# Prompt attention scores from rounded parts: queries and keys divided in two, three products for one

## The chip, the cores and the metric

The kernel runs on one core of a Trainium2 chip. The metric is the device time of one execution in microseconds; the kernel before takes 1125.41 us, the median of three runs (1124.91 to 1126.1). "Faster" and "slower" in this document mean a difference that such a measurement can tell from none.

The engines are named as in the profile: PE is TensorE (PEld its weight loads), DVE is VectorE, ACT is ScalarE, POOL is GpSimd, SP is SyncE, which here only issues transfers.

## The reference, cut to what matters

One layer of a hybrid decoder runs for a prompt of 512 tokens (with 16 learned meta tokens ahead of it) and for eight samples of 8 new tokens. Everything is float32. The change touches only the scores of the prompt's differential attention: four heads, two maps of 64 dimensions each.

```python
DA_HEADS = 4; DA_HEAD_DIM = 64; Q_BLOCK = 128; N_META = 16; SEQ = 512

def diff_attn_prompt(q, k, v, lam):            # q, k: (1, 528, 4, 2, 64)
    ...
    def one_block(args):                       # one block of 128 queries
        q_blk, start = args                    # q_blk is q * 64 ** -0.5
        q_pos = start + jnp.arange(Q_BLOCK)
        s = jnp.einsum('bqhmd,bkhmd->bhmqk', q_blk, k, preferred_element_type=jnp.float32)
        s = jnp.where(k_pos[None, :] <= q_pos[:, None], s, -jnp.inf)
        pr = jax.nn.softmax(s, axis=-1)
        a = pr[:, :, 0] - lam * pr[:, :, 1]    # the difference of the two maps
        return jnp.einsum('bhqk,bkhe->bqhe', a, vf)
```

The queries and keys come out of one input projection, h = rmsnorm(x) @ w_in, whose next columns give the values, the gated DeltaNet's inputs and the gates. After the attention follow the DeltaNet's chain, the merge of the branches, an output projection and a ConvFFN. The new keys and values are outputs too.

## The kernel before

**Rounded parts.** Nearly all large products of this kernel are made from a format that TensorE takes in one instruction, fp32r (F32R in the code). A float32 array is divided into a rounded part and the rest: `split` (L330) casts on ScalarE (L331) and subtracts on VectorE or GpSimd (L332). `project` (L366) and its like then add three products in PSUM: rounded x rounded, rounded x rest, rest x rounded. Products of plain float32 operands are taken as two instructions each. In the profile both formats show as f32 in a matmul's form; the tile names tell them apart: xhi, xlo, whi, wlo are parts, qT and kT are plain float32.

**Queries (`da_queries`, L1243).** The embedded input lies in SBUF as parts, transposed, in two stretches of columns: 256 columns and the rest. For each of four heads a projection of 128 columns of w_in fills two PSUM banks, pa and pb. ScalarE copies them, times 0.125, into qT (L1259, L1260), a tile [128, 4, 512]: on partitions 0 to 63 the first map's dimensions, on 64 to 127 the second's. VectorE then takes the sample queries (qb, L1266) and meta queries (qm, L1270) out of pb. There are two banks of the kind "d" at this point, used in turn, and the next product that needs pb's bank waits for the last of these reads. After the fourth head that is a product of `gdn_scalars` (L619; its weight tile is named baz in the profile), and its results go through a chain of small operations on VectorE, ScalarE and GpSimd. Then the work of `da_main` begins.

**Keys and values (`da_keys`, L1302).** Per head two projections, keys and then values, each in two halves of columns copied by ScalarE into a tile kvt (L1312). For the keys GpSimd copies kvt into kT (L1316 for the prompt's 512 columns, L1317 for the 16 meta columns; kT holds the meta columns first, 528 in all) and into kTm and kTs. TensorE transposes kvt into natural order, VectorE puts that into kno and knt (two buffers each), and GpSimd's queue issues the output transfers from there (L1336 to L1339).

**Scores (`prompt_rows`, L1422).** A head has four blocks of 128 queries; block i sees n = 16 + 128 (i + 1) keys. The cuts are 144, 272 and 400 columns for blocks 0 to 2, and 400 and 128 for block 3. For each cut one PSUM tile ps_m of two banks, one bank a map, takes the two products, each on a tile of 64 rows of the array. The tile ps_m has one buffer. VectorE reads it with a custom operation (L1372) that adds the mask and keeps the row maximum; ScalarE takes the exponential (L1448), VectorE forms the difference of the maps (L1457), TensorE transposes it (aT) and multiplies it with the values.

**What sets the order.** Generators yield at points where they could be interrupted; `merge` (L296) always continues the stream that has had the smallest part of its total. `mm` (L286) counts the work of each product:

```python
n = math.prod(rhs.shape[1:])
self.work += (1.68e-3 if lhsT.dtype == F32 and lhsT.shape[1] > 32 else 0.42e-3) * n
```

`prompt_attention` of a head and `da_keys` of the next ones are dealt out against each other (totals 37.6 and 70), with at most two heads' keys alive (KEYS = 2); together they are the main stream. Beside it runs `rest`: the attention of the samples over their cached pages (page tiles loaded by SP, transposed by TensorE into KT, L1541), then the gates. The delays in DELAY are in the same unit of work. On each engine the framework's scheduler then orders instructions once more by their readiness, and adds the waits.

**SBUF pools.** opool holds oa and ob, the outputs of the two branches, through the first half of the kernel; the pool da holds qT, kT, kno, knt and the attention's tiles until `da_main` has ended.

Of the kernel before, what the change touches and what calls it, by code (L numbers as in the profile page):

```python
# [9 lines left out]
F32 = mybir.dt.float32  # L10
F32R = mybir.dt.float32r
I32 = mybir.dt.int32
AF = mybir.ActivationFunctionType
ALU = mybir.AluOpType
# [4 lines left out]
SEQ = 512  # L19
NM = 16  # L20
# [5 lines left out]
H = 4  # L26
# [8 lines left out]
NQ = SEQ + NS + 2  # L35
NT = SEQ + NS + NM
CS = SEQ
CM = SEQ + NS
# [110 lines left out]
KEYS = 2  # L149
# [17 lines left out]
class Body:  # L167
# [39 lines left out]
    def run(self):  # L207
        nc, ctx = self.nc, self.ctx
# [13 lines left out]
        with ExitStack() as sm:  # L222
            with ExitStack() as s1:
                self.opool = self.pool(s1, "opool")
                self.oa = self.t(self.opool, [128, H, NQ], "oa")
                self.ob = self.t(self.opool, [128, H, NQ], "ob")
                with ExitStack() as s2:
# [17 lines left out]
                    def main():  # L245
                        head = {}
                        yield from self.da_main(dpool, self.gdn_project(0, head))
                        da.close()
                        self.chain = True
                        self.psum_g = self.pool(ctx, "psum_g", space=PSUM)  # L250
                        with ExitStack() as s:
                            self.gpool = self.pool(s, "gpool")
                            yield from self.gdn(head)
                        yield from self.mix_parts(self.pool(s2, "mix"))
                        self.wo0 += self.wout_tiles(self.pool(swo, "wo0", side="right"), 0)
# [987 lines left out]
    def da_queries(self, pool, first):  # L1243
        nc, keep, a, o = self.nc, self.keep, self.a, self.o
        w = a["w_in"][0]
        self.qT = self.t(pool, [128, H, SEQ], "qT")
        self.kTm = self.t(pool, [128, H, NM], "kTm")
# [7 lines left out]
        for h in range(H):  # L1255
            wt, out = first[h] if h < len(first) else (self.weight(w, C_Q + 128 * h), [])
            (pa, ca), (pb, cb) = out + self.dense(wt, self.x, HALF_Q[len(out) :])
            b0 = cb[0]
            nc.scalar.activation(self.qT[:, h, 0 : ca[1]], pa, AF.Copy, scale=0.125)  # L1259
            nc.scalar.activation(self.qT[:, h, b0:SEQ], pb[:, : SEQ - b0], AF.Copy, scale=0.125)  # L1260
            for m in range(2):
# [40 lines left out]
    def da_keys(self, pool, h, res):  # L1302
        nc, a, o = self.nc, self.a, self.o
        w = a["w_in"][0]
        for part, c0 in ((0, C_K), (1, C_V)):
# [8 lines left out]
            if part == 0:  # L1314
                kT = self.t(pool, [128, NM + SEQ], "kT", bufs=KEYS)
                nc.gpsimd.tensor_copy(kT[:, NM:], full[:, 0:SEQ])  # L1316
                nc.gpsimd.tensor_copy(kT[:, 0:NM], full[:, CM:NT])  # L1317
                nc.gpsimd.tensor_copy(self.kTm[:, h], full[:, CM:NT])
                nc.gpsimd.tensor_copy(self.kTs[:, h, :], full[:, CS:CM])
# [4 lines left out]
            self.transpose(p2[:NTL, :128], full[:, CS:NT])  # L1324
            nat = self.t(pool, [128, 4, 128], "kno" if part == 0 else "v", bufs=2 if part == 0 else KEYS)
            if part == 0:
                tail = self.t(pool, [128, 128], "knt", bufs=2)
                op = o["new_k_prompt"][0, 0, :, h].rearrange("t m d -> t (m d)")
# [50 lines left out]
    def meta_attention(self, pool):  # L1379
# [9 lines left out]
        self.transpose(tp[:NM, :128], S)  # L1389
        pT = self.t(pool, [128, 1, 128], "pTm")  # L1390
        nc.vector.tensor_copy(pT[64:80, 0], tp[:NM, :128])
# [6 lines left out]
        os = self.t(pool, [32, 1, 128], "oM")  # L1398
        pv = self.t(pool, [128, 128], "pvm")
        nc.vector.tensor_scalar(pv, acc[:, :128], rs, None, op0=ALU.mult)  # L1400
# [21 lines left out]
    def prompt_rows(self, pool, h, st, on, order):  # L1422
# [3 lines left out]
        for i in order:  # L1426
# [4 lines left out]
            for lo, hi in cuts:  # L1431
                p = self.t(self.psum_m, [128, 2, 512], "ps_m", bufs=1)[:, :, : hi - lo]
                for m in range(2):
                    r = slice(64 * m, 64 * m + 64)
                    self.mm(p[:, m], self.qT[r, h, 128 * i : 128 * i + 128], kT[r, lo:hi], start=True, stop=True)
                for m in range(2):
# [967 lines left out]
```

## Time and profile before

| | |
|---|---|
| median of three runs | 1125.41 us (1124.91 to 1126.1) |
| span of the profiled execution, first to last instruction | 1122.1 us |
| TensorE busy in the span | 1100.6 us, 98% |
| VectorE, ScalarE, GpSimd busy | 731.3 us, 524.7 us, 224.9 us |
| mean granted TensorE clock | 0.999 of full speed |
| embedding | 0 to 19 us |
| queries | 19 to 41 us |
| keys, values, prompt scores, part of the sample attention | 41 to 205 us |

The profile gives one execution; its span of 1122.1 us is the only time of that execution that the page holds, 3.3 us below the median of the runs. A group of instructions is one line: line of the code, engine, operation, output and inputs, forms, count; after the bar the busy time of the group, the mean duration of one in ns, and the engine's idle time ahead of them with what ended it. A matmul's form 64*128 64x400 is 64 rows and 128 columns of the array, and 400 columns streamed. Matmuls overlap in the pipe: the step from one start to the next tells what one costs, its duration does not. In the timeline a row has the start, the duration of the stretch, and "xN" for N instructions merged into it.

### The profile page before, as it was taken

How to read it: one execution, taken by the hardware profiler on the slowest of the kernel's cores; microseconds unless marked ns; L12 is line 12 of the kernel's file. 1: busy time of each engine (PE TensorE's matmuls, PEld its weight loads, DVE VectorE, ACT ScalarE, POOL GpSimd, SP SyncE). 2: the span in 40 equal slices, each digit the busy share in tenths (PEclk: the TensorE clock that was granted, in tenths of full speed). 3: DMA queues.
4: the chain of work that ended last, by engine and by line, in shares of the span. 5: the costliest groups of instructions: out<-in, count | busy, mean ns of one | idle time of the engine just before them, and what ended most of it. 6: DMA issues, size and time to landing. Idle time of an engine off the chain costs nothing.

```text
span 1122.1 us, 22894 instructions
## 1 busy us (share of the span) xinstructions
PE 1100.6 (98%) x8350; PEld 972.3 (87%) x8350; DVE 731.3 (65%) x1893; ACT 524.7 (47%) x1264; POOL 224.9 (20%) x336
## 2 busy tenths in 40 slices
PE   8999999999999999999999999999999999999997
PEld 7887797787787787799999987899999999988886
DVE  6456667695594477575344665599999999752315
ACT  6344444464464465452433244465555555832311
POOL 3231220210110110010000003344445454200000
PEclk9999999999999999999999999999999999999999
DMA  7385426847846856723234354323323332333213
GB/s 204 76 269 167 130 65 201 265 134 253 262 151 217 300 172 226 246 74 76 57 97 131 86 169 138 112 80 87 104 86 104 87 105 76 115 113 103 86 47 122
DMA packets 167354, 156.93 MB, mean 140 GB/s; under 512 B 12307, under 2 KB 123458, under 8 KB 167241
## 3 DMA queue, kind: packets, MB, share of 16 engines
q1 hardware_dynamic: 162833, 147.08, 42.8%
q0 software_dynamic: 3008, 5.16, 1.6%
q10 hardware_dynamic: 1400, 3.22, 0.9%
q8 instruction: 66, 1.08, 0.4%
q14 instruction: 47, 0.39, 0.1%
HBM read 145.54 MB, written 9.88 MB: 139 GB/s over the span
## 4 chain that ended last, share of the span: by engine, by line
PE 81%; DVE 8%; issue 3%; DMA 3%; ACT 2%; POOL 2%; SPq 0%; DVEq 0%; ACTq 0%; POOLq 0%
PE ps_d L289 30%; PE ps_t L289 22%; PE ps_g L289 16%; PE ps_s L289 6%; PE ps_t L437 6%; DVE cy L775 1%; DMA wraw<-in_w_out 1%; PE ps_m L289 1%; POOL grr L401 1%; DVE wlo L332 1%; DMA x<-in_x_prompt 1%; DVE row L1112 0%; ACT KT L1541 0%; DVE row L1113 0%; DVE xc L1114 0%
## 5 line engine op out<-in xcount | busy, mean ns | idle before, releaser
L289 PE MATMUL ps_d<-xhi,whi 128*128 128x256 f32 (+2 forms) x696 | 213.7, 310 | 0.1
L289 PE MATMUL ps_d<-xhi,wlo 128*128 128x256 f32 (+2 forms) x696 | 208.8, 303 | 1.5 <-DVE wlo L332 1.5
L332 DVE TENSOR_TENSOR wlo<-wraw,whi 128x512 fp32r<-128x512 f32 x190 | 143.2, 772 | 101.5 <-ACT whi L331 99.5
L289 PE MATMUL ps_d<-xlo,whi 128*128 128x256 f32 (+2 forms) x696 | 208.0, 302 | 0.0
L331 ACT CAST whi<-wraw 128x512 fp32r<-128x512 f32 x190 | 113.7, 621 | 167.2 <-PE ps_d L289 72.0
L289 PEld LDWEIGHTS ps_d<-xhi,whi 128*128 128x128 f32 x696 | 130.8, 189 | 5.9 <-issue 3.5
L289 PEld LDWEIGHTS ps_d<-xhi,wlo 128*128 128x128 f32 x696 | 130.5, 189 | 3.7 <-DVE wlo L332 2.0
L289 PEld LDWEIGHTS ps_d<-xlo,whi 128*128 128x128 f32 x696 | 131.1, 190 | 2.3 <-issue 2.0
L1541 ACT COPY KT<-ps_t 128x512 f32<-128x512 f32 x106 | 57.3, 601 | 34.3 <-PE ps_t L437 32.3
L332 DVE TENSOR_TENSOR lw<-sw,hw 128x512 fp32r<-128x512 f32 x76 | 69.8, 919 | 5.2 <-ACT hw L331 5.2
L437 PE MATMUL ps_t<-consts,page 128*128 128x128 f32 x512 | 68.1, 279 | 0.8 <-DMA page<-in_cache_k 0.6
L289 PE MATMUL ps_t<-fhit,hw 128*128 128x290 f32 x228 | 68.2, 299 | 0.1
L437 PEld LDWEIGHTS ps_t<-consts,page 128*128 128x128 f32 x512 | 55.6, 140 | 14.2 <-issue 7.8
L289 PE MATMUL ps_t<-fhit,lw 128*128 128x290 f32 x228 | 67.7, 297 | 0.0
L289 PE MATMUL ps_t<-flot,hw 128*128 128x290 f32 x228 | 67.7, 297 | 0.0
L331 ACT CAST hw<-sw 128x512 fp32r<-128x512 f32 x76 | 46.7, 617 | 18.3 <-PE ps_g L289 12.4
L289 PEld LDWEIGHTS ps_t<-fhit,hw 128*128 128x128 f32 x228 | 43.1, 189 | 0.3 <-DVE p L2069 0.3
L289 PEld LDWEIGHTS ps_t<-flot,hw 128*128 128x128 f32 x228 | 43.3, 190 | 0.0
L289 PEld LDWEIGHTS ps_t<-fhit,lw 128*128 128x128 f32 x228 | 43.2, 189 | 0.0
L2044 ACT ACTIVATE fy<-fpre,fw 128x592 f32<-128x592 f32 x22 | 19.5, 885 | 46.4 <-DVE fpre L2004 46.4
L2046 DVE SCALAR_TENSOR_TENSOR fy<-fpre,fw,fy 128x592 f32<-128x592 f32 x44 | 36.5, 830 | 1.0 <-ACT fy L2044 0.4
L289 PE MATMUL ps_s<-KT,qb 128*32 128x256 f32 x512 | 34.0, 385 | 0.6
(722 smaller groups left out, 2861.0 us busy)
## 6 DMA issues: line engine op xcount, KB each, us to landing
page<-in_cache_k SPq DMA_DIRECT2D x128, 256.0 KB, 4.2
page<-in_cache_v SPq DMA_DIRECT2D x128, 256.0 KB, 4.2
wraw<-in_w_in SPq DMA_DIRECT2D x86, 256.0 KB, 3.2
wraw<-in_w_ffn_in SPq DMA_DIRECT2D x50, 256.0 KB, 3.0
wraw<-in_w_down SPq DMA_DIRECT2D x44, 256.0 KB, 2.9
raw<-in_w_ffn_in SPq DMA_DIRECT2D x38, 256.0 KB, 3.0
wraw<-in_w_out SPq DMA_DIRECT2D x16, 256.0 KB, 3.1
x<-in_x_prompt SPq DMA_DIRECT2D x4, 512.0 KB, 7.0
```

What stands on the lines that cost most here:

```text
L289: return self.nc.tensor.matmul(out, lhsT, rhs, **kw).ins
L331: self.nc.scalar.copy(hi, raw)
L332: (eng or self.nc.vector).tensor_tensor(out=lo, in0=raw, in1=hi.bitcast(F32), op=ALU.subtract)
L401: nc.gpsimd.tensor_tensor(out=dst, in0=dst, in1=self.mhalf[:rows, :n], op=ALU.pow)
L437: self.nc.tensor.transpose(out, in_, self.ident[:k, :k])
L775: nc.vector.scalar_tensor_tensor(out=y, in0=pre[:, j : j + n], scalar=self.cw[:, ch, 24 + j : 25 + j], in1=y, op0=ALU.mult, op1=ALU.add)
L1541: copy(kt[:, :, 128 * j : 128 * j + 128], tp)
L2044: nc.scalar.activation(y, pre[:, 0:592], AF.Identity, bias=fw[:, m, 19:20], scale=fw[:, m, 16:17])
L2046: nc.vector.scalar_tensor_tensor(out=y, in0=pre[:, j : j + 592], scalar=fw[:, m, 16 + j : 17 + j], in1=y, op0=ALU.mult, op1=ALU.add)
```

## The change

The prompt's queries and keys are held as parts, and the scores are made from three products of parts in place of one float32 product.

- Queries: ScalarE's scaled copies go to a rounded tile qT, and VectorE computes 0.125 p - rounded into a second tile qlo. This tile takes the place of ob in opool; ob itself is allocated after `da_main`.
- Keys: GpSimd's two copies into kT are replaced by `split` into two tiles (ScalarE's cast, VectorE's subtraction for the prompt's 512 columns; ScalarE's cast, GpSimd's subtraction for the 16 meta columns).
- Scores: for each cut three products per map, the two maps in turn inside each; six matmuls in place of two products.
- Room: kno and knt have one buffer in place of two, and the meta attention's pT and pv share the tags knt and hjunk.

```diff
-                self.ob = self.t(self.opool, [128, H, NQ], "ob")
+                self.qlo = self.t(self.opool, [128, H, NQ], "ob", F32R)
...
                         yield from self.da_main(dpool, self.gdn_project(0, head))
+                        self.ob = self.t(self.opool, [128, H, NQ], "ob")
...
-        self.qT = self.t(pool, [128, H, SEQ], "qT")
+        self.qT = self.t(pool, [128, H, SEQ], "qT", F32R), self.qlo
...
-            nc.scalar.activation(self.qT[:, h, 0 : ca[1]], pa, AF.Copy, scale=0.125)
-            nc.scalar.activation(self.qT[:, h, b0:SEQ], pb[:, : SEQ - b0], AF.Copy, scale=0.125)
+            for p, c in ((pa, slice(0, ca[1])), (pb[:, : SEQ - b0], slice(b0, SEQ))):
+                hi, lo = (e[:, h, c] for e in self.qT)
+                nc.scalar.activation(hi, p, AF.Copy, scale=0.125)
+                nc.vector.scalar_tensor_tensor(
+                    out=lo, in0=p, scalar=0.125, in1=hi.bitcast(F32), op0=ALU.mult, op1=ALU.subtract
+                )
...
-                kT = self.t(pool, [128, NM + SEQ], "kT", bufs=KEYS)
-                nc.gpsimd.tensor_copy(kT[:, NM:], full[:, 0:SEQ])
-                nc.gpsimd.tensor_copy(kT[:, 0:NM], full[:, CM:NT])
+                kT = [self.t(pool, [128, NM + SEQ], f"kT{p}", F32R, bufs=KEYS) for p in ("hi", "lo")]
+                for d, c, eng in ((slice(NM, None), slice(0, SEQ), nc.vector), (slice(0, NM), slice(CM, NT), nc.gpsimd)):
+                    self.split(kT[0][:, d], kT[1][:, d], full[:, c], eng)
...
-            nat = self.t(pool, [128, 4, 128], "kno" if part == 0 else "v", bufs=2 if part == 0 else KEYS)
+            nat = self.t(pool, [128, 4, 128], "kno" if part == 0 else "v", bufs=1 if part == 0 else KEYS)
             if part == 0:
-                tail = self.t(pool, [128, 128], "knt", bufs=2)
+                tail = self.t(pool, [128, 128], "knt", bufs=1)
...
-        pT = self.t(pool, [128, 1, 128], "pTm")
+        pT = self.t(pool, [128, 1, 128], "knt", bufs=1)
...
-        pv = self.t(pool, [128, 128], "pvm")
+        pv = self.t(pool, [128, 128], "hjunk", bufs=1)
...
-                for m in range(2):
-                    r = slice(64 * m, 64 * m + 64)
-                    self.mm(p[:, m], self.qT[r, h, 128 * i : 128 * i + 128], kT[r, lo:hi], start=True, stop=True)
+                for j, (qp, kp) in enumerate(((0, 0), (0, 1), (1, 0))):
+                    for m in range(2):
+                        r = slice(64 * m, 64 * m + 64)
+                        self.mm(
+                            p[:, m], self.qT[qp][r, h, 128 * i : 128 * i + 128], kT[kp][r, lo:hi], start=j == 0, stop=j == 2
+                        )
```

## The prediction, made before the changed kernel was run

> **What bounds the kernel now.** I read the first page from the top, then the stage in which the change lies, then single instructions. The page first: engines, TensorE by slices, the chain of waits.
>
> ```profile
> PE 1100.6 (98%) x8350; PEld 972.3 (87%) x8350; DVE 731.3 (65%) x1893; ACT 524.7 (47%) x1264; POOL 224.9 (20%) x336
> ...
> PE 81%; DVE 8%; issue 3%; DMA 3%; ACT 2%; POOL 2%; SPq 0%; DVEq 0%; ACTq 0%; POOLq 0%
> PE ps_d L289 30%; PE ps_t L289 22%; PE ps_g L289 16%; PE ps_s L289 6%; PE ps_t L437 6%; DVE cy L775 1%; DMA wraw<-in_w_out 1%; PE ps_m L289 1%; POOL grr L401 1%; DVE wlo L332 1%; DMA x<-in_x_prompt 1%; DVE row L1112 0%; ACT KT L1541 0%; DVE row L1113 0%; DVE xc L1114 0%
> ```
>
> TensorE is busy for 98% of the span and makes 81% of the chain: it is the bound. But the score product (ps_m) is 1% of the chain. So no matter how well its matmuls shrink, the prize is a few microseconds of 1122. What counts is TensorE's occupation by score groups, and whatever makes TensorE wait in their stage. The next rows are the stage from the key projections to the last score (busy times in the order PE, PEld, DVE, ACT, POOL), and the score matmuls themselves.
>
> ```profile
> 41.00:205.00 164.00, 160.59 (x1339) 132.62 (x1331) 103.62 (x400) 75.00 (x204) 35.93 (x75) 1.00 0.52 161
> ```
> ```profile
> L289 PE MATMUL ps_m<-kT,qT x80: 271/442/601, 70.1 to 200.8; 64*128 64x400 f32 x32, 64*128 64x128 f32 x16, 64*128 64x272 f32 x16, 64*128 64x144 f32 x16
> ```
>
> The 80 records are 40 products (4 heads, 5 cuts, 2 maps), two instructions each. VectorE is 63% busy there, ScalarE 46%.
>
> **What a score group costs now.** These are timeline rows around one cut of 400 columns and one of 128 (start, duration), and of rounded products of 256 columns.
>
> ```profile
> 74.08 0.32 PE L289 MATMUL ps_d<-xhi,whi 128*128 128x336 f32 x1
> 74.23 0.32 PE L289 MATMUL ps_d<-xlo,whi 128*128 128x336 f32 x1
> ...
> 74.63 0.30 PEld L289 LDWEIGHTS ps_m<-kT,qT 64*128 64x128 f32 x4 [0.21 <-issue]
> 74.63 0.94 PE L289 MATMUL ps_m<-kT,qT 64*128 64x400 f32 x4
> ...
> 75.50 0.19 PEld L289 LDWEIGHTS ps_d<-xhi,whi 128*128 128x128 f32 x1 [0.57 <-issue]
> ```
> ```profile
> 72.48 0.49 PE L289 MATMUL ps_m<-kT,qT 64*128 64x128 f32 x4
> 72.90 0.42 PE L289 MATMUL ps_d<-xhi,wlo 128*128 128x336 f32 x1
> ```
> ```profile
> 200.28 0.28 PE L289 MATMUL ps_d<-xlo,whi 128*128 128x256 f32 x1
> 200.40 0.28 PE L289 MATMUL ps_d<-xhi,wlo 128*128 128x256 f32 x1
> ```
>
> From its first load to the next instruction a group holds TensorE 0.87 us at 400 columns and 0.42 at 128: 1.65 ns a column plus 0.21 fixed (first load, and emptying the array before the tile shape changes back). Both maps fit in that, so their tiles of 64 rows run at once. 272 and 144 columns follow as 0.66 and 0.45.
>
> Rounded products start 0.15 us apart at 336 columns and 0.12 at 256: some 0.45 ns a column, with a floor near 0.11 that I take to be the weight load. The four loads of the group above are over in 0.30 us while its matmuls have only begun, so loads hide behind the other tile pair's streaming.
>
> **The change part by part.**
>
> *Score matmuls.* Each map's two-instruction product becomes three products. If they run at the spacings above, pairwise, a group is 0.11 (first load) + 2 spacings + the last stream + 0.10 (emptying). 400 columns: 0.11 + 0.18 + 0.18 + 0.17 + 0.10 = 0.74, 0.13 less. 272: 0.11 + 0.126 x 2 + 0.12 + 0.10 = 0.58, 0.08 less. 144 and 128 sit on the load's floor: 0.11 + 0.12 x 2 + 0.06 + 0.10 = 0.51, 0.06 and 0.09 more. A head has two cuts of 400 and one of each other: -0.26 - 0.08 + 0.15 = -0.19, four heads -0.8.
>
> Three groups are not run whole today; other streams' transposes stand between their two maps:
>
> ```profile
> 96.35 0.94 PE L289 MATMUL ps_m<-kT,qT 64*128 64x400 f32 x2
> 97.22 1.53 PE L437 MATMUL ps_t<-consts,page 128*128 128x128 f32 x12
> ...
> 98.97 0.94 PE L289 MATMUL ps_m<-kT,qT 64*128 64x400 f32 x2
> ```
> ```profile
> 129.07 0.94 PE L289 MATMUL ps_m<-kT,qT 64*128 64x400 f32 x2
> ...
> 130.74 0.94 PE L289 MATMUL ps_m<-kT,qT 64*128 64x400 f32 x2
> ```
> ```profile
> 194.80 0.72 PE L289 MATMUL ps_m<-kT,qT 64*128 64x272 f32 x2
> ...
> 198.05 0.72 PE L289 MATMUL ps_m<-kT,qT 64*128 64x272 f32 x2
> ```
>
> One map alone holds TensorE as long as both together (96.35 to 97.22 is 0.87), so a split group saves twice: another 0.13 + 0.13 + 0.08 = 0.34. Sum on TensorE: -1.1. No row shows a rounded matmul under 256 columns or on 64 rows. Upper bound: the narrow cuts stream as slowly as the four-byte products (1.65 ns a column for each of the three); lower bound: their spacing follows the columns (0.06). That is +3.0 and -1.0 over four heads against my floor. I take the floor, as every wide row lies near 0.45 ns a column.
>
> [...]
>
> *Queries.* The two scaled copies per head stay on ScalarE; VectorE gets 8 subtractions that read PSUM. The rows at the end of the last head:
>
> ```profile
> 39.85 0.38 ACT L1260 ACTIVATE qT<-ps_d 128x256 f32<-128x256 f32 x1
> ...
> 41.28 0.16 DVE L1270 TENSOR_SCALAR qm<-ps_d 64x2 f32<-64x2 f32 x1
> ...
> 41.58 1.34 PE L289 MATMUL ps_d<-xhi,baz 128*32 128x336 f32 x16 [0.33 <-DVE qm L1270]
> 42.19 0.42 DVE L730 COPY bat<-ps_d 128x256 f32<-128x256 f32 x1
> ```
>
> A VectorE instruction on 256 PSUM columns is 0.42 (last row). Seven of the eight lie under a projection that keeps TensorE busy. The eighth stands in VectorE's queue before qb and qm of the same bank, and the next product already waits 0.33 for that bank: **+0.4** on the path. Behind it on VectorE stand the key weights' rest and bat, late by the same 0.4, not again.
>
> *Keys.* Per head GpSimd loses two copies; ScalarE gets a cast of 512 and one of 16, VectorE a subtraction of 512, GpSimd one of 16. The nearest rows:
>
> ```profile
> L1316 POOL COPY kT<-kvt x4: 636/792/1878, 53.7 to 146.9; 128x512 f32<-128x512 f32 x4
> ```
> ```profile
> L332 DVE TENSOR_TENSOR wlo<-wraw,whi 128x512 fp32r<-128x512 f32 x29 | 19.8, 687 | 12.5 <-ACT whi L331 11.5 <-DMA page<-in_cache_k 0.4 <-issue 0.4
> ```
> ```profile
> L331 ACT CAST whi<-wraw 128x512 fp32r<-128x512 f32 x29 | 17.8, 620 | 23.2 <-PE ps_d L289 20.2 <-issue 1.9 <-DMA wraw<-in_w_in 1.1
> ```
>
> ScalarE: 4 x (0.62 + 0.2) = 3.3 us more, where 0.2 is an estimate for 16 columns from the 0.38 of the row with 256; VectorE: 4 x 0.69 = 2.8. The key's own lateness, about 1 us, costs nothing: the first copy starts at 53.7 and the first score at 70.1, and later heads' keys are made a head ahead. What counts is whom the queues hold up: the evacuations of page transposes (KT) and of attention transposes (aT), and weight casts. TensorE's largest waits for them in this stage:
>
> ```profile
> PEld ps_t L437 <- ACT KT L1541: 1.2, 3, 0.7
> PEld ps_t L437 <- ACT aT L1464: 1.1, 3, 0.4
> PEld ps_s L289 <- ACT oa L1420: 0.9, 1, 0.9
> ```
>
> They make 3.2 us for 75.0 us of ScalarE work, or 4%. 4% of 6.1 added microseconds is 0.25; waits grow faster than load, so I take twice that, **+0.5**. Bounds: 0, and 6.1 if TensorE waited for all of it. GpSimd gets lighter.
>
> *Buffers.* One key buffer for the output instead of two, shared tags and ob in the place of qlo: heads' keys are some 30 us apart (four copies from 53.7 to 146.9), far more than an output DMA needs. Cost 0; if that cover were gone, a head's wait for its DMA.
>
> *Sum.* -1.1 + 0.4 + 0.5 = -0.2 us. The page gives the profiled execution's span, 1122.1 us, and no other time of its own; the runs' median of 1125.41 lies 3.3 above. The difference is laid on the median: **1125.2 us**.
>
> **The rivals.** About 0.2%, 2.25 us, is what a measurement tells from no change.
>
> *Narrow cuts stream four times slower* (slower). Place: the cuts of 144 and 128, 24 product pairs. Price: +3.0 as bounded above, so 1128.2. It turns the result to slower once such a pair takes 0.22 us instead of 0.12 (24 x 0.10 = 2.4, and -0.2). For: every rounded matmul here has at least 256 columns, so nothing refutes it. Against: the even rate of the rows shown.
>
> *Split groups become whole* (faster). The maps now alternate inside each product, and the scheduler may keep them together. Three second visits vanish, at the new cost 0.74 x 2 + 0.58 = 2.1: 1123.1. Against: the second map still waits for its own PSUM half, which is likely what splits them today.
>
> *Loads are not hidden* (slower). The second and third product of a map load new weights into the rows where the one before still streams; if such a load has to wait for the stream's end, every product pays 0.11 + its stream. 400: 3 x (0.11 + 0.17) + 0.10 = 0.94; 272: 0.79; 144 and 128: about 0.61 and 0.59. A head is then +0.14 + 0.13 + 0.16 + 0.17 = +0.6, all +2.4; with +0.9 for the waits 1128.7. The 0.30 us for four loads speak against it. [...]
>
> *The change doesn't do what it says: rounded tiles of 64 don't pair.* Six streams in a row, 0.21 + 6 x 0.18 = 1.29 at 400, are +0.42 for 8 cuts; 272 gives 0.97, +0.31 for 4; the narrow ones 0.93, +0.5 for 8: +8.6, with the waits 1134.9. Both maps' instructions do pair today, on the same rows.
>
> Besides, the planner counts the score products at 0.42 for 1.68 per product, so streams are dealt out in another order; this moves each case by up to some 2 us (TensorE's idle time in the stage is 164.0 - 160.6 = 3.4).
>
> **How the numbers follow.** Forecast 0.52 (faster 0.09, same 0.36, slower 0.07 by the order alone); narrow cuts 0.22 (same 0.05, slower 0.17); whole groups 0.12 (faster 0.09, same 0.03); loads 0.06 (same 0.01, slower 0.05); no pairing 0.03 (slower); other orders 0.05 (0.02, 0.01, 0.02). Together faster 0.20, same 0.46, slower 0.34. The range 1121.0 to 1130.3 reaches from the whole groups to the narrow cuts, each with 2.1 of order beyond it. The forecast's own is 1123.1 to 1127.3.
>
> **What would show it.** Right: six score matmuls a group, 0.74 us to the next instruction at 400 columns and about 0.51 at 144; a wait near 0.75 before the first product after the queries; ScalarE 3 us and VectorE 6 busier up to 205 us. Wrong: narrow groups of 0.85 or more, loads that start after their predecessor's stream, maps that start one after the other, a wait for kT or kno, or a stage that changes its length after 205 us, where nothing was edited.

## The result, and the profile after

The changed kernel takes **1136.33 us** (median of four runs, 1133.12 to 1138.04), the kernel before beside it 1125.16 (1124.47 to 1126.1): a ratio of 1.0094, 95% interval 1.0082 to 1.0106. It is slower by 11 us, where 1125.2 was forecast, and outside the range. The profiled execution is the slowest of the four, 1138.04 us with a span of 1136.3, 14.2 above the span before. In this and in every later profile the span lies 1.7 to 1.8 us below that execution's time, so the span before (1122.1) belongs to an execution of some 1123.9 us, an estimate, 1.3 to 1.5 under the medians of that kernel; that is one reason why 14.2 is more than the 11.2 between the medians.

From the page of the changed kernel, engines and chain of waits. Its line numbers lie 1 to 8 above those of the kernel before: the helpers mm, split and transpose are L290, L333 and L438.

```profile
PE 1112.3 (98%) x8390; PEld 980.2 (86%) x8390; DVE 738.4 (65%) x1905; ACT 528.0 (46%) x1272; POOL 218.4 (19%) x332
...
PE 81%; DVE 9%; DMA 3%; ACT 3%; issue 2%; POOL 1%; SPq 0%; DVEq 0%; ACTq 0%; POOLq 0%
```

The page alone hides the loss: shares are what they were. VectorE has 7.1 us more and ScalarE 3.3, as the working said (6 and 3.3), GpSimd 6.5 less. TensorE, which was to lose 1.1, is busy for 11.7 more.

The next rows are TensorE's timeline of the changed kernel, at the places that the prediction named. The rest of the queries shows under the tile name ob, whose room it takes.

```profile
41.67 1.34 PE L290 MATMUL ps_d<-xhi,baz 128*32 128x336 f32 x16 [0.54 <-DVE qm L1275]
...
73.08 0.33 PE L290 MATMUL ps_m<-kThi,qT 64*128 64x128 f32 x2
73.25 0.28 PE L290 MATMUL ps_m<-kTlo,qT 64*128 64x128 f32 x2
73.36 0.28 PE L290 MATMUL ps_m<-kThi,ob 64*128 64x128 f32 x2
73.56 0.42 PE L290 MATMUL ps_d<-xhi,wlo 128*128 128x336 f32 x1
...
74.69 0.45 PE L290 MATMUL ps_m<-kThi,qT 64*128 64x400 f32 x2
74.98 0.34 PE L290 MATMUL ps_m<-kTlo,qT 64*128 64x400 f32 x2
75.16 0.34 PE L290 MATMUL ps_m<-kThi,ob 64*128 64x400 f32 x2
75.43 0.42 PE L290 MATMUL ps_d<-xhi,wlo 128*128 128x336 f32 x1
...
142.72 0.33 PE L290 MATMUL ps_m<-kThi,qT 64*128 64x128 f32 x2
142.89 0.27 PE L290 MATMUL ps_m<-kTlo,qT 64*128 64x128 f32 x1
143.84 0.59 PE L438 MATMUL ps_t<-consts,on 128*128 128x128 f32 x2 [0.68 <-DVE on L1494]
144.36 0.32 PE L290 MATMUL ps_m<-kTlo,qT 64*128 64x128 f32 x1
144.62 0.33 PE L438 MATMUL ps_t<-consts,on 128*128 128x128 f32 x1
144.88 0.32 PE L290 MATMUL ps_m<-kThi,ob 64*128 64x128 f32 x1
145.13 0.33 PE L438 MATMUL ps_t<-consts,on 128*128 128x128 f32 x1
145.39 0.32 PE L290 MATMUL ps_m<-kThi,ob 64*128 64x128 f32 x1
```

Where a group is run whole it costs what was worked out, or a little less: 0.74 us at 400 columns (74.69 to 75.43), 0.48 at 128. The weight loads of the second and third pair at 400 columns are these:

```profile
74.79 0.19 PEld L290 LDWEIGHTS ps_m<-kTlo,qT 64*128 64x128 f32 x2
74.98 0.19 PEld L290 LDWEIGHTS ps_m<-kThi,ob 64*128 64x128 f32 x2
```

Each begins while the pair before it is in the array, and the third pair starts 0.18 us behind the second (74.98 to 75.16). But not every group is whole any more. The one at 142.72 is six matmuls with four transposes of the tile on among them, and is spread over 2.7 us from its first start to its last. A *visit* below is a run of score matmuls with nothing else between them; the 20 groups were 23 visits before and are 31 now.

The last rows are stretches of the changed kernel's span: length, busy time of PE, PEld, DVE, ACT and POOL, the granted TensorE clock (PEclk), DMA share and GB/s.

```profile
41.00:219.00 178.00, 171.36 (x1399) 141.89 (x1396) 109.32 (x413) 81.00 (x225) 34.62 (x72) 0.98 0.51 156
47.38:50.79 3.41, 3.41 (x18) 3.41 (x17) 0.29 (x2) 1.62 (x3) 3.21 (x1) 0.50 0.00 0
146.36:149.78 3.42, 3.42 (x16) 2.73 (x15) 1.67 (x15) 1.92 (x5) 0.00 (x0) 0.50 0.00 0
252.18:255.59 3.41, 3.41 (x16) 3.35 (x15) 2.90 (x8) 0.63 (x2) 1.22 (x2) 0.50 0.30 76
```

Three stretches of 3.41 us run at half clock; in the first of them a product of 256 columns starts every 0.21 us (47.59 to 47.81), against 0.12 just ahead of it (47.15 to 47.27). Each is put at half its length, 5.1 us together, an estimate from the clock of 0.50. The profile before has none ahead of its last matmul. They are not all of the loss, and not in every execution: the fastest of the four, 1133.12 us, has a mean clock of 0.998 where the profiled one has 0.994, and is 8 us slow all the same. By the traces' start times the whole loss arises between 41 and 250 us: the last copy into oa is 2.3 us late (216.8 before, 219.1 after), the sample attention beside it 14.

The profiled runs can be taken apart roughly. *Half clock* is half the length of such stretches; *waits* are TensorE's idle times over 0.1 us between 41 and 520 us; *row changes* are successive matmuls, in the whole span, whose forms differ in the rows of the array, counted as 32, 64 or 128 (fewer rows go up to the next of these, a convention of this count). They are put at 0.19 us each, an estimate from a run below that measured it for one kind of product.

| | kernel before | changed kernel | us |
|---|---|---|---|
| last matmul starts at | 1115.5 | 1129.6 | +14.1 |
| half clock | 0 | 3 stretches | +5.1 |
| waits | 10.2 us | 13.7 us | +3.4 |
| row changes | 98 | 116 | +3.4 |
| score groups themselves | | | -1.0 |
| left over | | | +3.2 |

### The profile page after: what moved, and what is told of

It reads as the page before. It is cut to its first block, busy times and chain, and to the rows that moved or that the text cites. A ratio compares the mean times of both kernels' runs of the same rounds, so it can differ in the third digit from the quotient of the medians.

```text
span 1136.3 us, 22980 instructions
## 1 busy us (share of the span) xinstructions
PE 1112.3 (98%) x8390; PEld 980.2 (86%) x8390; DVE 738.4 (65%) x1905; ACT 528.0 (46%) x1272; POOL 218.4 (19%) x332
## 4 chain that ended last, share of the span: by engine, by line
PE 81%; DVE 9%; DMA 3%; ACT 3%; issue 2%; POOL 1%; SPq 0%; DVEq 0%; ACTq 0%; POOLq 0%
PE ps_d L290 31%; PE ps_t L290 20%; PE ps_g L290 16%; PE ps_s L290 7%; PE ps_t L438 6%; DVE wlo L333 1%; PE ps_m L290 1%; DMA wraw<-in_w_out 1%; DVE S L1377 1%; DMA wraw<-in_w_in 1%; DMA x<-in_x_prompt 1%; DMA wraw<-in_w_ffn_in 1%; ACT whi L332 0%; DVE lw L333 0%; POOL grr L402 0%
## 5 line engine op out<-in xcount | busy, mean ns | idle before, releaser
L290 PE MATMUL ps_d<-xhi,whi 128*128 128x256 f32 (+2 forms) x696 | 214.8, 311 | 0.7 <-DVE vn L924 0.6
L290 PE MATMUL ps_d<-xhi,wlo 128*128 128x256 f32 (+2 forms) x696 | 210.5, 306 | 2.2 <-DVE wlo L333 2.2
L290 PE MATMUL ps_d<-xlo,whi 128*128 128x256 f32 (+2 forms) x696 | 209.8, 305 | 0.0
L333 DVE TENSOR_TENSOR wlo<-wraw,whi 128x512 fp32r<-128x512 f32 x190 | 143.3, 772 | 101.2 <-ACT whi L332 99.5
L290 PEld LDWEIGHTS ps_d<-xhi,whi 128*128 128x128 f32 x696 | 132.3, 191 | 6.2 <-issue 1.9
L290 PEld LDWEIGHTS ps_d<-xhi,wlo 128*128 128x128 f32 x696 | 131.9, 191 | 5.4 <-DVE wlo L333 2.9
L290 PEld LDWEIGHTS ps_d<-xlo,whi 128*128 128x128 f32 x696 | 132.6, 192 | 1.2 <-issue 0.8
L333 DVE TENSOR_TENSOR lw<-sw,hw 128x512 fp32r<-128x512 f32 x76 | 68.6, 903 | 5.2 <-ACT hw L332 5.2
L438 PE MATMUL ps_t<-consts,page 128*128 128x128 f32 x512 | 68.4, 279 | 0.5 <-ACT on L1482 0.2
L290 PE MATMUL ps_t<-fhit,hw 128*128 128x290 f32 x228 | 68.1, 299 | 0.1
L438 PEld LDWEIGHTS ps_t<-consts,page 128*128 128x128 f32 x512 | 56.1, 141 | 13.6 <-issue 8.2
L290 PE MATMUL ps_t<-fhit,lw 128*128 128x290 f32 x228 | 67.7, 297 | 0.0
L290 PE MATMUL ps_t<-flot,hw 128*128 128x290 f32 x228 | 67.6, 297 | 0.0
L290 PEld LDWEIGHTS ps_t<-fhit,hw 128*128 128x128 f32 x228 | 43.1, 189 | 0.4 <-DVE p L2077 0.4
L290 PEld LDWEIGHTS ps_t<-flot,hw 128*128 128x128 f32 x228 | 43.2, 190 | 0.0
L290 PEld LDWEIGHTS ps_t<-fhit,lw 128*128 128x128 f32 x228 | 43.1, 189 | 0.0
L290 PE MATMUL ps_s<-KT,qb 128*32 128x256 f32 x512 | 36.9, 385 | 0.4
```

Of the source, the lines that this page charges most:

```text
L290: return self.nc.tensor.matmul(out, lhsT, rhs, **kw).ins
L333: (eng or self.nc.vector).tensor_tensor(out=lo, in0=raw, in1=hi.bitcast(F32), op=ALU.subtract)
L438: self.nc.tensor.transpose(out, in_, self.ident[:k, :k])
```

## The experiments

Each time is a median beside runs of the kernel before on the same chip (medians of these 1124.7 to 1125.6), and a loss is the distance to that median; the ratio carries its 95% interval.

**Engine work or score products.** Two kernels take one half of the change each. The first has the parts of queries and keys, the engines' added work and the buffers, but multiplies the rounded parts as float32, two products a cut:

```diff
+ qT[0], kT[0] read as float32: mm(p[:, m], qT[0][r, ...], kT[0][r, lo:hi], start=True, stop=True)
```

> Leaves out: the scores are two float32 products of the rounded parts alone, so the rests of queries and keys are made but not used. Everything else of the change is in (the extra casts and subtractions, one kno buffer, ob after qlo). TensorE's written order comes out with 23 visits to the score tiles, as before. Theory A (the loss comes from the order that the six matmuls bring: 31 visits in place of 23, more changes of the array's tile shape, and clock drops that follow): 1125 to 1127, no worse than the kernel before by more than the 0.2 us of the query bank and some waits for ScalarE. Theory B (the added casts and subtractions hold up ScalarE and VectorE, whom TensorE waits for): 1132 to 1137, nearly the whole loss. Theory C (the clock drops alone, by chance of their phase): any time, but with a mean clock under 0.997 where it is slow.

Measured: 1125.78, ratio 1.0004 (0.9995 to 1.0014). The second has queries and keys as before, in one rounded tile each, and takes three products of that same pair:

```diff
+ for j in range(3):
+     for m in range(2):
+         self.mm(p[:, m], self.qT[r, ...], kT[r, lo:hi], start=j == 0, stop=j == 2)
```

> Leaves out the rests: queries and keys are made as before, as one rounded tile each, and the same rounded pair is multiplied three times per map. So only the score matmuls of the change are in, and no added cast or subtraction. TensorE's written order has 31 visits to the score tiles. Theory A: 1130 to 1137, as slow as the changed kernel. Theory B: 1124 to 1126. Theory C: as A only where the clock is under 0.997.

Measured: 1135.38, ratio 1.0090 (1.0068 to 1.0111), with 31 visits. So the added engine work costs some 0.7 us, near the 0.9 of the prediction (0.4 for the bank and 0.5 for the load), and six matmuls in the place of two products bring nearly all of the loss (10.3 of 11.2 us), though the groups together are 1.0 us cheaper by their rows. The profiled run of this second kernel (1133.07 us) has no half-clock stretch ahead of its last matmul.

**Whole groups.** The second to sixth matmul of a group get a high priority, so the scheduler sets nothing between them (the two maps also change places inside each product); in a second kernel the planner's count of a group is brought back to its old value as well.

```diff
+ for m in (1, 0): ... with self.tc.high_priority():  # all but the group's first matmul
+ self.work += 2 * (1.68e-3 - 3 * 0.42e-3) * (hi - lo)   # second kernel alone
```

> The changed kernel, with the second to sixth matmul of each score group at a priority that lets nothing come between them: 20 visits to the score tiles instead of 31, all six matmuls in one. Theory A: 4 to 8 us below the changed kernel's 1136 (20 fewer changes of shape at about 0.2 us each way, and fewer clock drops), so 1127 to 1132. Theory B: 1135 to 1137, no change.

> As the run before, and the planner's count of a score group is kept at what it was for two float32 products, so that the streams are dealt out as before the change. 20 visits to the score tiles, and about as few runs of sample-attention matmuls as before. Theory A: near or below the kernel before, 1122 to 1126, since TensorE's own work is 1 us less. Theory B: 1134 to 1137.

Measured: 1133.37, ratio 1.0080 (1.0050 to 1.0111), and 1130.81, 1.0050 (1.0033 to 1.0067). Both have 20 visits and fewer row changes than the kernel before (94 and 92), and still lose 8.3 and 5.7 us, above what theory A gave them (1127 to 1132, 1122 to 1126). So the parted groups and their row changes are not the main thing. In the first the loss is there by 250 us, as in the changed kernel. In the second, these rows of the copies into oa and KT,

```profile
L1425 ACT COPY oa<-ps_t x4: 587/587/593, 107.9 to 216.3; 128x512 f32<-128x512 f32 x4
...
L1556 ACT COPY KT<-ps_t x106: 562/592/676, 59.2 to 440.8; 128x512 f32<-128x512 f32 x106
```

answer to these of the kernel before:

```profile
L1420 ACT COPY oa<-ps_t x4: 585/588/592, 108.2 to 216.8; 128x512 f32<-128x512 f32 x4
...
L1541 ACT COPY KT<-ps_t x106: 558/592/663, 59.1 to 434.9; 128x512 f32<-128x512 f32 x106
```

The prompt's attention ends 0.5 us early. Most of the loss comes 200 us behind it, in the DeltaNet's stage, of which nothing was edited.

**The planner's count alone.** What is left is the order. The count is changed to 0.75 of its value in the kernel *before*, to 1.25 in the same kernel, and kept as it was in the changed kernel.

```diff
 # kernel before, 0.75 and 1.25        # changed kernel, old count
+ self.work -= 2 * 0.42e-3 * (hi - lo)
+ self.work += 2 * 0.42e-3 * (hi - lo)
+ self.work += 2 * (1.68e-3 - 3 * 0.42e-3) * (hi - lo)
```

> The kernel before with its float32 score products, and one number changed: the planner counts a score group at 0.75 of what it was (2.52e-3 in place of 3.36e-3 a column), as it counts the six matmuls of the change. No arithmetic differs. In the order of the instructions on TensorE the score groups are then visited 25 times in place of 23. Theory D (the loss is in the dealing out of the streams by that count): this kernel alone already loses a good part, 1128 to 1132. Theory S (the loss comes from other streams that slip between the six matmuls of a group): 1124.5 to 1126.5. Both may hold in part; then some 1127.

> The kernel before with its float32 score products; the planner counts a score group at 1.25 of what it was (4.20e-3 a column), the same step as the run with 0.75 in the other direction. No arithmetic differs. 23 score visits, as before; at the weight split of the DeltaNet's stage, where TensorE waited 3.0 us in the run with 0.75, the order on TensorE is as in the kernel before (products of 336 columns and a run of 16 KT,qb stand ahead of the one that waits). Theory O (the order before lies at a good spot, and any step away from it costs): 1129 to 1135. Theory L (what costs is the lower count, which lets the main stream run ahead of the sample attention): 1123 to 1127.

> The change in full, but the planner's count of a score group is kept as before (3.36e-3 a column); the six matmuls of a group stay free to be parted. 25 visits in place of 31. Theory D: close to before, 1125 to 1128, since the streams are dealt out as before. Theory S: as slow as the change less the few visits, 1131 to 1135. Against the kernel with whole groups and the old count (1130.8): if this one is no slower, the parting of the groups is not what costs.

Measured: 1135.77, ratio 1.0093 (1.0075 to 1.0110); 1136.63, 1.0113 (1.0096 to 1.0129); 1133.62, 1.0078 (1.0060 to 1.0096). **This is the core of the case.** One number in the planner, with no arithmetic changed, costs as much as the whole change, and it does so in either direction. With the old count the change still loses 8.1 us, so the count is not the only way to a bad order: the scheduler behind it finds another one too. Each theory on *one* property of the order (parted groups, the lower count) expected one of these runs near 1126, and missed there; theory S meets the last run (1131 to 1135) but fails at 0.75. The parted groups do have a share: keeping them whole lowers the loss from 11.2 to 8.3 us with the new count and from 8.1 to 5.7 with the old, though the intervals of each pair overlap.

Here is one place of the loss, some 5 of the 11.5 us by which the last matmul is late with 0.75 (most of the rest is there by 250 us), on TensorE's timeline of that kernel:

```profile
407.34 0.63 PE L289 MATMUL ps_s<-KT,qb 128*32 128x256 f32 x6
...
408.65 0.32 PE L289 MATMUL ps_d<-xlo,whi 128*128 128x336 f32 x1
412.00 0.58 PE L289 MATMUL ps_d<-xhi,wlo 128*128 128x256 f32 x1 [3.03 <-DVE wlo L332]
```

and in the kernel before:

```profile
404.07 0.32 PE L289 MATMUL ps_d<-xlo,whi 128*128 128x336 f32 x1
404.32 1.07 PE L289 MATMUL ps_s<-KT,qb 128*32 128x256 f32 x16
406.89 0.39 PE L289 MATMUL ps_d<-xhi,wlo 128*128 128x256 f32 x1 [1.50 <-DVE wlo L332]
```

Both wait for the same rest of weights. Before, the 16 products KT,qb stand right ahead of the waiting one and cover 1 us; with the other count they have run already, the wait is 3.0 us, and a half-clock stretch of twice 3.41 us begins in it (410.95 to 417.77, clock 0.50). The changed kernel with the old count, and the one with whole groups and the old count, have the same wait (3.03 and 3.02) and one half-clock stretch of 3.41 us.

With 1.25 that wait is gone, but the DeltaNet's chain is bare 60 us later, where more than half of the 12.3 us arises by which its last matmul is late:

```profile
465.94 0.45 PE L289 MATMUL ps_g<-gv,dtbig_up 80*80 80x128 f32 x2
467.39 0.49 PE L289 MATMUL ps_g<-gS,kk 128*128 128x128 f32 x2 [1.00 <-DVE gS L990]
468.32 0.49 PE L289 MATMUL ps_g<-grhs,xy 128*128 128x128 f32 x2 [0.44 <-DVE grhs L1023]
469.16 0.49 PE L289 MATMUL ps_g<-gv,kn 128*128 128x128 f32 x2 [0.35 <-ACT gv L1033]
```

In the kernel before, weight products of other streams stand between these steps, and none of them waits:

```profile
462.14 0.45 PE L289 MATMUL ps_g<-gv,dtbig_up 80*80 80x128 f32 x2
462.34 0.37 PE L289 MATMUL ps_d<-xhi,wlo 128*128 128x256 f32 x1
...
462.67 0.42 PE L289 MATMUL ps_g<-gS,kk 128*128 128x128 f32 x2
```

**Whole groups without the change.** The kernel before, with the second map of each group kept right behind the first (20 visits).

```diff
+ for m in (1, 0): ... with self.tc.high_priority():  # the group's second product
```

> The kernel before with float32 score products, the second map of each group kept right behind the first (20 visits in place of 23). Nothing else is edited. If whole groups are worth what the prediction gave them, three visits of 0.87 us at most, the time is 1123.5 to 1125. If keeping groups whole pushes other streams' work out of its order (theory O: any change of order here costs, since the order before is the one that its delays fit), it is slower, 1127 to 1131.

Measured: 1125.92, ratio 1.0005 (0.9995 to 1.0015). That lies between the two forecasts: the three saved visits are worth nothing that can be seen, and this new order is as good as the old one, so not every change of order costs.

**Other counts, other places.** Whole groups with a count of 3.72e-3 or 3.24e-3 a column, and with the old count and one head's gate weights divided at high priority.

```diff
+ self.work += 2 * 0.6e-3 * (hi - lo)      # or 0.36e-3
+ if h == 1: s.enter_context(self.tc.high_priority())   # third kernel, around split_w in gdn_gate
```

> The change with whole groups (20 visits) and the planner's count of a group raised beyond the old one (3.72e-3 a column). In its order TensorE changes its tile shape a little less often than before (174 to 180 changes by the same count). Theory T (the number of tile changes sets the loss, some 0.2 us each, plus clock windows): 1123 to 1127. Theory O (any new order costs, also by waits in the DeltaNet's stage behind): 1129 to 1134, as the kernel with the old count (1130.8).

> The change with whole groups (20 visits), the planner's count of a group at 3.24e-3 a column in place of the old 3.36e-3. In this order the run of 16 KT,qb and products of 336 columns stand ahead of the product that waits for the weights' rest in the DeltaNet's stage, as in the kernel before. Theory W (of the 5.7 us that the kernel with whole groups and the old count lost, some 4.5 are that one wait, 3.0 in place of 1.5 us, and the clock window behind it): 1125 to 1127.5. Theory O (loss turns up elsewhere with every new order): 1129 to 1133.

> The kernel with whole groups and the old count (1130.8) with one edit: the gate weights of the second head are divided at high priority. That moves the order behind it: the run of 16 KT,qb stands right ahead of the product that waits for the weights' rest, as before, though fewer products of 336 columns do. Same two theories: W gives 1125 to 1128, O 1129 to 1133.

Measured: 1132.01, ratio 1.0060 (1.0042 to 1.0079); 1131.01, 1.0059 (1.0042 to 1.0076); 1137.20, 1.0107 (1.0090 to 1.0124). The theory of the tile changes falls with the first (92 row changes, 98 before), the theory of the one wait for the weights' rest with the other two: their order leaves 0.0 and 0.5 us of that wait, and more than half of the loss arises between 435 and 506 us instead, the stretch in which the DeltaNet's chain is bare in the run with 1.25. The last of the three is slower than either theory allowed.

**The price of a change of rows, and the clock.** 144 matmuls in six blocks behind the queries of the kernel before, their results not used.

```diff
+ for pair in ((full, full), (top, top), (top, low), (full, top), (full, thin), (full, full)):
+     for j in range(24): matmul(p[...], hi[r, 0, :c], hi[r, 1, :256], start=True, stop=True)  # r, c = pair[j % 2]
```

> The kernel before, with 144 matmuls put in behind the queries whose result is not used: six blocks of 24, each fp32r, 256 columns streamed; 128 rows throughout; 64 rows throughout; rows 0 to 63 and 64 to 127 in turn; 128 and 64 rows in turn; 128 and 32 weight columns in turn; 128 rows throughout again. Theory T (a change of the tile's shape costs some 0.2 us): the blocks of one shape take 24 x 0.12 = 2.9 us, those in turn 24 x 0.32 = 7.7. If changes are free, all take 2.9, or less where two row tiles run at once (1.5). The kernel's time grows by the sum, some 25 us or 17.

1154.53 us in one execution, 29.6 more than the kernel before beside it. Stretches inside four blocks; the count behind PE's busy time takes in matmuls that reach over an end of the stretch, so the steps named below are from start to start on the timeline:

```profile
36.40:39.30 2.90, 2.90 (x24) 2.84 (x24) 0.52 (x4) 0.00 (x0) 0.00 (x0) 1.00 0.40 96
43.95:45.10 1.15, 1.15 (x4) 0.66 (x4) 0.00 (x0) 0.00 (x0) 0.00 (x0) 1.00 0.00 0
46.10:55.20 9.10, 9.10 (x19) 5.12 (x18) 0.00 (x0) 0.00 (x0) 0.00 (x0) 0.50 0.00 0
55.90:58.60 2.70, 2.70 (x14) 2.42 (x14) 0.00 (x0) 0.00 (x0) 0.00 (x0) 0.50 0.02 6
```

With 128 rows throughout a matmul starts every 0.12 us. With 128 and 64 rows in turn it is every 0.31 at full clock (second row) and 0.51 at half (third): **0.19 us a change of rows**. 128 and 32 weight columns in turn cost nothing (fourth row, at half clock every 0.21, as products of one shape have it in the half-clock stretch at 47.38 of the changed kernel; 0.117 back at full clock). Two row tiles at once were not seen: the scheduler pulled that block apart. And though TensorE was busy without a gap, the clock fell to one half (0.50) from 45.16 to 58.81 us; at half that length, 6.8 of the 29.6 are put down to it.

**The good order with rounded products.** A group takes its first product twice, the second time over the first, and so stands like the old group in length and count.

```diff
+ for j, (qp, kp) in enumerate(((0, 0), (0, 0), (0, 1), (1, 0))):
+     for m in (1, 0): ...  # whole as above; start=j < 2, stop=j in (0, 3)
```

> The change with its groups whole and with the first product of each map taken twice (the second time it overwrites the first), so a group has eight rounded matmuls in place of six. By its length and by the planner's count (8 x 0.42e-3 is the old 3.36e-3 a column) it stands like the old group, and the order on TensorE is, but for 33 of 7268 other matmuls, that of the kernel before with whole groups (1125.9). More work on TensorE than the change has: a group of 400 takes 0.74 + 0.18 = 0.92, 272 0.69, 144 and 128 0.61, over four heads +2.0 against the float32 groups and +2.7 against the change; with the other engines' +0.7 the sum is 1128.5. Theory O (the loss is the order alone): 1127 to 1130, faster than the change in spite of the added products. Theory M (six or more rounded matmuls cost more in their surroundings than their rows show, whatever the order): 1135 or more.

Measured: 1132.60, ratio 1.0064 (1.0047 to 1.0081): faster than the change, with two matmuls more a group, but 2.6 us above the upper end of the theory of the order, and 2.4 below what theory M asked for. That is 6.7 above its model (7.3, each against its own runs of the kernel before), of which 2.7 were worked out for matmuls and engines. The few instructions that did move show where another 2.6 go. TensorE's timeline of this kernel:

```profile
105.67 0.27 PE L290 MATMUL ps_m<-kThi,ob 64*128 64x128 f32 x2
107.73 1.18 PE L438 MATMUL ps_t<-consts,on 128*128 128x128 f32 x4 [1.78 <-DVE on L1500]
108.55 0.56 PE L290 MATMUL ps_d<-xhi,whi 128*128 128x256 f32 x1
```

and of its model, the kernel before with whole groups:

```profile
104.45 0.49 PE L289 MATMUL ps_m<-kT,qT 64*128 64x128 f32 x4
104.87 0.39 PE L289 MATMUL ps_d<-xhi,whi 128*128 128x256 f32 x1
...
105.69 0.28 PE L289 MATMUL ps_d<-xhi,whi 128*128 128x256 f32 x1
106.89 0.30 PE L437 MATMUL ps_t<-consts,on 128*128 128x128 f32 x1 [0.91 <-DVE on L1489]
```

Seven products that stood ahead of the transposes of on have moved behind them. The wait grows by 0.9 us, and 3.41 us from 107.46 on run at half clock, another 1.7. The remaining 1.4 to 2.0 us are not accounted for.

**Covering that wait.** The change with whole groups (1133.37), and one delay set later for each head: the transposes of on fall due 2.2 or 3.6 units behind the normalisation instead of 1.49.

```diff
 # DELAY[h][23], all four heads
- 1.49
+ 2.2        # second kernel: 3.6
```

> The change with whole groups (1133.4 before this edit) and one delay changed for each head: the transposes of the normalised outputs (tile on) are due 2.2 of the planner's units behind the normalisation in place of 1.49, so other products may stand ahead of them. Behind some 470 us the order on TensorE is the one of the kernel before. Theory O (the loss is waits that an order leaves uncovered, for on first of all, and the clock windows behind them; none of it belongs to the rounded products): a good part comes back, 1126 to 1130. If nothing comes back (1132 to 1136), the wait for on isn't a main place of the loss.

> As the run with 2.2, with 3.6 units in place of 1.49; the order on TensorE is that of the kernel before from about 420 us on, with other work ahead of the on transposes of most heads. Theory O: 1125 to 1129, and no wait for on over 1 us behind the first two heads. Otherwise 1132 to 1136.

Measured: 1131.58, ratio 1.0069 (1.0051 to 1.0087), above its expectation; 1127.44, 1.0025 (1.0014 to 1.0036), within it. One delay gives back nearly 6 of the 8 us, with the change's own products and its planner's count. TensorE's waits ahead of the four heads' transposes of on are 1.82, 0.96, 1.36 and 1.27 us with whole groups alone; with 2.2 the first three stay as they were and the last falls to 0.45, and with 3.6 none but 0.27, 0.44 and 0.91 are left. So 2.2 was too little to cover them. But TensorE's idle time as a whole is nearly the same with 2.2 and with 3.6 (11.9 and 11.7 us between 41 and 520 us), so other waits have come in their place.

By the traces this kernel and the changed one hold the same instructions, every kind in the same number (engine, operation, tiles and form); only their order differs. The changed kernel loses 11.2 us and this one 2.7: **8.4 us are the order alone.** The kernel is still 2.7 us behind the old one; the profiled run has one half-clock stretch (47 to 50 us) and 1.5 us of waits more. No version was found that beats the kernel before.

## Why the prediction was wrong

Point by point, by its own steps:

- **Score matmuls, -1.1: right for the products themselves,** -1.0 where -0.8 was forecast. 0.74, 0.57, 0.49 and 0.48 us were measured for whole groups of 400, 272, 144 and 128 columns (0.74, 0.58, 0.51, 0.51 forecast), so the three rivals on the products themselves (narrow cuts slow, loads not hidden, no pairing) fall. In the rows shown no load waits for the end of the stream before it: the loads at 74.79 and 74.98 go to rows through which the pair before still streams, and a pair of 400 columns takes 0.18 us. The floor near 0.11 us stands in the rows (twelve transposes of 128 columns in 97.22 to 98.60 before, 0.115 each; a pair of 128 columns after, 73.25 to 73.36); that it is the weight load, and that the fixed 0.21 us of a group are a first load and an emptying of the array, was the author's estimate. What a run measured is 0.19 us for a change of rows. The other 0.34, for three parted groups, was worth nothing that can be seen (1125.92 with whole groups in the kernel before).
- **Query bank, +0.4: too large.** The wait grew from 0.33 to 0.54 us, half of that.
- **Keys' engine load, +0.5, and buffers, 0: borne out, as far as the noise lets one see.** Both and the bank make 0.7 us (interval -0.6 to +1.6) in the kernel with the parts alone, where 0.9 was forecast. The doubling from 0.25 to 0.5 was the author's estimate; no run shows that waits grow faster than load. The keys' transfers out of kno land 2.9 to 6.8 us after their issue in the changed kernel (2.8 to 7.3 before), with some 30 us from head to head (four issues from 64.5 to 155.6).
- **Split groups become whole, a rival: the opposite came.** A group of six matmuls can be parted in five places, one of two products in one: 31 visits instead of 23, and 25 with the old count.
- **The order: the step that failed.** "This moves each case by up to some 2 us (TensorE's idle time in the stage is 164.0 - 160.6 = 3.4)". The count alone moved the kernel before by +10.2 and +11.7 us, and the change's own instructions in two orders lie 8.4 us apart. As a rival of its own, another order had been given 0.05 of the chances. The bound was wrong in kind. Idle time that *is* there limits what a better order can win; it says nothing on what a worse one can lose, which is cover that the profile before counts as busy time. And the bound was taken in one stage, while the dealing out by this count runs on into the next: in the four kernels with whole groups of six and a count set anew, more than half of the loss falls behind 390 us. In the changed kernel itself it is there by 250 us.

What is shown: a change in the order alone can cost as much as the loss (0.75 and 1.25), the added engine work does not (parts alone), and 8.4 of the 11.2 us come back by order alone (whole groups and the later delay, the same instructions). For the rounded products and the engines' work in themselves that leaves 2.7, unless the order with 3.6 is a better one than the old. The pieces seen are bare waits, half-clock stretches and, in the change itself, row changes. What stays open: why each order loses just what it does. In the slower kernels 1 to 7 us of the profiled span fit none of the three pieces (in one the pieces sum to 1.6 too much). Up to 1.8 of that lies in the profile before, whose execution was under its median: the two kernels that are as fast as the old one (parts alone, and whole groups without the change) have 1.8 and 1.6 of it too. The profiled run with 2.2 (1129.76 us) has no half-clock stretch and is 5 us slow, of which its waits explain 1.7. The same products in exactly the old order were not run.

## What to carry to other kernels

Before an edit is priced by its instructions, look whether it changes a number that a planner or scheduler orders by; if so, price the order first, by changing that number alone. A bound on a worse order comes from the work that now covers waits, not from the idle time that is left. And keep a short sequence that must not be parted together by priority rather than by luck, then look at what it displaced.

## What the runs showed of the hardware

- **The clock fell without an idle stretch.** Ahead of the last matmul, the half-clock stretches shown here last 3.41 us, or twice that (410.95 to 417.77 with the count at 0.75), or four times (45.16 to 58.81 in the run with blocks). In the changed kernel they start on a grid of 3.413 us, a step worked out from their starts: 47.38, 146.36 and 252.18 lie 29.0 and 31.0 such steps apart. In the 3.41 us ahead of these three TensorE was busy for 3.41, 2.73 and 1.95 us, and ahead of the stretch in the run with blocks (41.75 to 45.16) for all 3.41, with products on 64 rows throughout and, from 43.88 on, on 128 and 64 rows in turn. Nearly the same stretch of small products behind the queries (43.97 to 47.38, busy for 3.41 us in both kernels) is followed by a half-clock stretch in the changed kernel and by none in the kernel before. What makes the clock fall is not shown here, and busy time alone doesn't tell it: in the changed kernel 241.94 to 245.35, on the same grid, is busy for 2.00 us only, and full clock follows.
- **A change of rows cost 0.19 us, a change of weight columns nothing**, for rounded products of 256 columns at full clock in the run with blocks: a matmul started every 0.31 us with 128 and 64 rows in turn and every 0.117 with 128 and 32 weight columns in turn, against 0.12 with one shape.
- **Rounded products on 64 rows kept the rate of those on 128**: a pair of 400 columns takes 0.18 us (74.98 to 75.16 in the changed kernel), 0.45 ns a column, and a product of 336 columns on 128 rows 0.15 (74.29 to 74.44), 0.45 too. A pair of 128 columns takes 0.11 us (73.25 to 73.36), so it is no faster than a product of 256 columns on 128 rows (0.12).
